# Hybrid S5/NATTEN/PEER layer: a third pair of split weight buffers, and the chunk states laid out chunk by chunk

## The chip, the cores and the metric

The kernel runs on one core of one Trainium2 chip. The metric is the device time of one execution in microseconds, taken as the median of several executions; a profile is one further execution, recorded by the hardware profiler. Engines are named as in the profile: PE (TensorE, matmul; PEld its weight loads), DVE (VectorE), ACT (ScalarE), POOL (GpSimd), SP (SyncE, which issues DMAs). `mm`, `mc`, `kk`, `yy` and `tp` are PSUM banks.

## What is computed

One layer on 512 latent tokens of width 1024, with 256 context tokens, in float32: a modulated RMSNorm; one wide projection `w_in` into u (512), k, v, q (512 each) and two gates (1024 each); a bidirectional S5 state space mixer on u beside a neighbourhood attention on q, k, v; a gated merge; then a PEER layer that gathers experts from tables.

```python
hx = modulate(x, p['norm1_g'], shift1, scale1)
hc = modulate(ctx, p['norm1_g'], mod_c[0], mod_c[1])
px = hx @ p['w_in']
u_x, k_x, v_x, q_x, ga_x, gb_x = jnp.split(px, [COL_K, COL_V, COL_Q, COL_GA, COL_GB], axis=-1)
pc = hc @ p['w_in'][:, :(IN_COLS if with_ctx_out else CTX_COLS)]
y_ssm_x, y_ssm_c = s5_mixer(u_x, u_c, p, with_ctx_out)
branch_a = (s5_glu(y_ssm_x, p) @ p['w_branch_a']).astype(x.dtype)
branch_b = na_mixer(q_x, k_x, v_x, kc, vc, p['na_rpb']) @ p['w_branch_b']
merged = jax.nn.sigmoid(ga_x) * branch_a + jax.nn.sigmoid(gb_x) * branch_b
x = x + gate1 * (merged @ p['w_out'])
x = x + gate2 * peer_ffn(modulate(x, p['norm2_g'], shift2, scale2), ...)
return rms_norm(x, final_g)
```

The S5 mixer is a linear recurrence of 32 groups with 64 complex states each, forward and backward, context tokens first. The kernel cuts the 768 tokens into 96 chunks of 8 (32 of context, 64 latent), makes each chunk's end state, and carries the states from chunk to chunk.

## The kernel before

**Matmuls in split precision.** Every weight tile (128 columns, up to 8 blocks of 128x128) is loaded into `wraw`, copied by ACT into `whi` (rounded to fp32r, L174) and the rest taken by DVE into `wlo` = `wraw` - `whi` (L175). A product is then three matmuls: `whi` with the high part of the input, `whi` with its low part, `wlo` with the high part (L445 to L447; 128x512 for the latent tokens into `mm`, 128x256 for the context into `mc`). `wseq` lists all tiles in the order of use: 16 of `win` (u 0 to 3, k 4 to 7, v 8 to 11, q 12 to 15), then those of the merge in the order of the string MERGE, then the later ones. `w_next` gives out the next tile and, through `w_ahead`, starts the loads two tiles ahead and the split one tile ahead. There are three `wraw` and two each of `whi` and `wlo` (`wbufs`).

**Stages.** (1) u: projections 0 to 3, `u_out` writes them to DRAM in chunk order, `x_load` reads them back as X. (2) Block E, `e_part`: 16 sets of four matmuls from X and the matrices FT, each copied out of PSUM by three ACT copies into E (L552 to L554; forward states in partitions 0 to 63, backward ones in reversed order in 64 to 127). (3) Block K, `k_prep` and `g_outer`: outer products on DVE (`Gc`, L330 to L335), matmuls `kk`, `yy` (L518, L521), ACT copies into `ks` (L524), and six stores each from `ks` to Kd in DRAM on SP's queue (L528 to L530). (4) The sweep, `carry`: 12 calls of four DVE instructions (L612 to L615) that carry the states in E over distances of 1, 2, 4, 8, 16 chunks; beside it PE runs the k, v and q projections, whose results ACT copies into kTC (L563 to L572), `vb`, V (L640) and q (L654). (5) S: four ACT copies of the latent chunks of E (L643, L644). (6) Attention and `y_part`, which uses S. (7) The merge: gates, branches, GLU, beside 32 products `jk` for the second modulation (`mod2`, L816, each with a transfer `wm2`, two buffers; the first modulation's rest on `wm`). (8) PEER.

**Layout of E.** It is [128, 2, 32, 97]: real and imaginary part, group, then chunk, chunk innermost. A carry of distance d = 1, 2, 4 ... reads and writes every 2nd, 4th, 8th ... chunk. The multiplier `lam` is broadcast over the chunks.

**What sets the order.** The whole program is put in order by a scheduler that simulates a timeline (`schedule_with_timeline_sim`); SP's order is written by hand. Each engine runs its own queue in that order. Pools are stacks from the two sides of SBUF: a pool that is opened takes the place of those closed before it, and its first use waits for theirs. `gst2` (with `Gc`, `ks`) is closed at the end of block K; `scp` (with `lam`, `ta`, `tb_`) is opened then.

Of the kernel before, what the change touches and what calls it, by code (L numbers as in the profile page):

```python
# [23 lines left out]
KD = 8  # L24
# [4 lines left out]
G = 32  # L29
# [57 lines left out]
def tile_hybrid(ctx, tc, A, out, dbg=None):  # L87
# [66 lines left out]
    wseq += [("wq", i, KD) for i in range(2 * NH)]  # L154
    wseq += [("puT", j, KD) for j in range(UA, 128)]
    mark = [None]
    wraw, wsp = {}, {}
    wext = {}
    wcnt = {}

    def wtile(kind, dt):
        n, x = wbufs[kind]
        c = wcnt[kind] = wcnt.get(kind, -1) + 1
        if wext and c % (n + x) >= n:
            return wext[0].tile([128, KD, 128], dt, tag=kind, name=kind, bufs=x)
        return wst.tile([128, KD, 128], dt, tag=kind, name=kind, bufs=n)
# [3 lines left out]

    def w_split(raw, kn, eng):
        hi = wtile("whi", F32R)
        lo = wtile("wlo", F32R)
        act.copy(hi[:, :kn], raw[:, :kn])  # L174
        i = eng.tensor_sub(lo[:, :kn], raw[:, :kn], hi[:, :kn].bitcast(F32))  # L175
        if eng is gp:
            mark[0] = i.ins
        return hi, lo

    def w_ahead(load_to, split_to, eng):  # L180
        while wpos[0] < min(load_to, len(wseq)):
            i = wpos[0]
            src, m, kn = wseq[i]
            w = wtile("wraw", F32)
            sy.dma_start(w[:, :kn].rearrange("p k c -> p (k c)"), A[src][m])
            wraw[i] = w
            wpos[0] += 1
        while wpos[1] < min(split_to, len(wseq)):
            i = wpos[1]
            wsp[i] = w_split(wraw.pop(i), wseq[i][2], eng)  # L190
            wpos[1] += 1

    def w_next(want, eng=gp):
# [292 lines left out]
    ecm, ep = open_pool(name="ep", bufs=1, side="right")  # L486
    E = ep.tile([128, 2, G, NCK + 1], F32, name="E")
    dve.memset(E[:, :, :, 0:1], 0.0)

# [54 lines left out]
    def e_part(m):  # L544
        for r in range(2):
            for q in (0, 4):
                g0 = 8 * m + q
                p = bank()
                for i in range(4):
                    pe.matmul(p[:, i * NCK:(i + 1) * NCK], FT[m][:, q + i, r], X[:, g0 + i], start=True, stop=True)  # L550
                pv = p[:, :4 * NCK].rearrange("p (g c) -> p g c", c=NCK)
                act.copy(E[0:64, r, g0:g0 + 4, 1:], pv[0:64])  # L552
                act.copy(E[64:128, r, g0:g0 + 4, 1:1 + CC], pv[64:128, :, CC - 1::-1])
                act.copy(E[64:128, r, g0:g0 + 4, 1 + CC:], pv[64:128, :, NCK - 1:CC - 1:-1])  # L554

# [45 lines left out]
    def carry(l, first, step, n):  # L601

        ta = scp.tile([128, 2, G, 31], F32, name="ta", tag="ta", bufs=1)[:, :, :, 0:n]
        tb_ = scp.tile([128, 2, G, 31], F32, name="tb_", tag="tb_", bufs=1)[:, :, :, 0:n]
        d = 1 << l
        to = E[:, :, :, first:first + (n - 1) * step + 1:step]
        fr = E[:, :, :, first - d:first - d + (n - 1) * step + 1:step]

        def bc(j):
            return lam[l][:, j].rearrange("p r (g o) -> p r g o", o=1).to_broadcast([128, 2, G, n])  # L610

        dve.tensor_tensor(ta, fr, bc(0), op=ALU.mult)  # L612
# [791 lines left out]
```

## Time and profile before

| | |
|---|---|
| median of 3 runs | 1843.59 us (1843.41 to 1844.24) |
| profiled execution, its own time | 1847.01 us |
| its span | 1845.2 us |
| mean granted PE clock of it | 0.968 |
| PE busy | 1724.4 us (93%) |
| DVE busy | 1468.6 us (80%) |
| ACT busy | 782.4 us (42%) |
| POOL busy | 372.9 us (20%) |

The span is the profiled execution from first to last instruction; its own time has the launch around it. A busy PE is one that has a matmul under way; the granted clock says at which part of full speed (2.4 GHz is 1.00, 1.2 GHz 0.50). In the page's list of what ended last PE holds 64% of the span, DVE 18%, DMA 9%. On times of the first stages: blocks E and K lie at about 88 to 133 us, the sweep with the k, v and q projections at 133 to 222, attention to about 311, the merge to about 432.

### The profile page before, as it was taken

What the parts mean: (1) busy time and instruction counts of PE and PEld (TensorE: products, weight loads), DVE (VectorE), ACT (ScalarE), POOL (GpSimd) and SP (SyncE); (2) the same over time, 40 slices, a digit from 0 to 9 for tenths busy, and PEclk for the clock granted to TensorE, in tenths of its full rate; (3) what the DMA queues carried; (4) which work ended last, traced back from release to release, by engine and by line L of the source; (5) the groups of instructions that cost most, each with busy time, mean ns of one, the idle gap of its engine ahead of it and who ended that gap; (6) DMA issues with size and microseconds to landing.
All of it is one profiled execution on the core that took longest, in us unless ns stands there. A gap on an engine that the chain in (4) does not pass through costs nothing.

```text
span 1845.2 us, 27478 instructions
## 1 busy us (share of the span) xinstructions
PE 1724.4 (93%) x9941; PEld 1507.5 (82%) x9941; DVE 1468.6 (80%) x3041; ACT 782.4 (42%) x1220; POOL 372.9 (20%) x304
## 2 busy tenths in 40 slices
PE   5999899899999899995589999999999999999997
PEld 2878677777799799994579899999999999988885
DVE  8889765875689998999888788888878788794455
ACT  6452555432464346665423333333333333333333
POOL 0001000000000000000332344544445444440012
PEclk9999999999999999995699999999999999999998
DMA  8341362885634336765799799999999999994332
GB/s 332 95 134 59 97 170 49 282 285 164 210 130 149 115 121 187 209 196 166 228 392 348 266 344 354 323 340 342 331 337 350 341 328 344 327 337 138 127 114 80
DMA packets 186328, 426.16 MB, mean 231 GB/s; under 512 B 25552, under 2 KB 91216, under 8 KB 186192
## 3 DMA queue, kind: packets, MB, share of 16 engines
q1 hardware_dynamic: 84816, 231.44, 37.1%
q0 software_dynamic: 36864, 134.23, 20.2%
q10 hardware_dynamic: 64512, 58.73, 10.2%
q8 instruction: 78, 1.28, 0.3%
q14 instruction: 58, 0.48, 0.1%
HBM read 388.72 MB, written 35.62 MB: 230 GB/s over the span
## 4 chain that ended last, share of the span: by engine, by line
PE 64%; DVE 18%; DMA 9%; issue 5%; POOL 2%; ACT 2%; SPq 0%; ACTq 0%; DVEq 0%; POOLq 0%
PE acc L1276 8%; PE acc L1275 8%; PE acc L1277 8%; PE kk L447 4%; PE yy L445 4%; PE yy L447 4%; PE yy L446 4%; PE kk L446 4%; PE kk L445 4%; DVE wlo L175 3%; DMA wm<-in_wmodT_dram 3%; PE mm L445 2%; PE mm L447 2%; DMA gu<-in_pu_dram,idx 2%; PE mm L446 2%
## 5 line engine op out<-in xcount | busy, mean ns | idle before, releaser
L174 ACT CAST whi<-wraw 128x1024 fp32r<-128x1024 f32 (+1 forms) x212 | 213.8, 1009 | 222.6 <-PE mm L446 100.4
L1158 POOL DMA_INDIRECT gu<-in_pu_dram,idx x128 | 168.9, 1319 | 598.0 <-PE mm L1142 385.3
L175 DVE TENSOR_TENSOR wlo<-wraw,whi 128x1024 fp32r<-128x1024 f32 (+1 forms) x212 | 247.6, 1169 | 36.1 <-ACT whi L174 35.5
L1158 POOL DMA_INDIRECT gu<-in_pv_dram,idx x128 | 176.8, 1382 | 192.1 <-DVE gacc L1176 165.8
L1176 DVE SCALAR_TENSOR_TENSOR gacc<-gu,av,gacc 128x1024 f32<-128x1024 f32 x127 | 162.7, 1281 | 28.1 <-DMA gu<-in_pv_dram,idx 27.7
L1257 DVE TENSOR_TENSOR wlo<-wraw,whi 128x1024 fp32r<-128x1024 f32 x128 | 157.6, 1232 | 33.5 <-ACT whi L1256 33.0
L1165 DVE SCALAR_TENSOR_TENSOR gj<-gu,hrow 128x1024 bf16<-128x1024 f32 x128 | 156.2, 1220 | 33.9 <-DMA gu<-in_pu_dram,idx 33.8
L447 PE MATMUL kk<-hth,wlo 128*128 128x384 f32 x512 | 174.2, 340 | 3.4 <-DVE wlo L175 3.4
L445 PE MATMUL kk<-hth,whi 128*128 128x384 f32 x512 | 173.4, 339 | 2.4 <-ACT ring L956 2.4
L445 PE MATMUL yy<-hth,whi 128*128 128x384 f32 x512 | 173.0, 338 | 1.5 <-ACT whi L174 1.3
L446 PE MATMUL kk<-htl,whi 128*128 128x384 f32 x512 | 173.1, 338 | 0.0
L447 PE MATMUL yy<-hth,wlo 128*128 128x384 f32 x512 | 173.0, 338 | 0.0
L446 PE MATMUL yy<-htl,whi 128*128 128x384 f32 x512 | 172.4, 337 | 0.0
L1256 ACT CAST whi<-wraw 128x1024 fp32r<-128x1024 f32 x128 | 133.7, 1046 | 59.5 <-PE kk L446 26.7
L1144 ACT ACTIVATE gs<-mm 128x512 f32<-128x512 f32 x96 | 94.1, 1090 | 56.1 <-PE mm L1142 53.1
L447 PE MATMUL mm<-hxh,wlo 128*128 128x512 f32 x256 | 103.3, 404 | 11.4 <-DVE wlo L175 11.4
L445 PE MATMUL mm<-hxh,whi 128*128 128x512 f32 x256 | 101.6, 402 | 5.6 <-ACT whi L174 3.0
L446 PE MATMUL mm<-hxl,whi 128*128 128x512 f32 x256 | 102.5, 400 | 0.0
L447 PEld LDWEIGHTS kk<-hth,wlo 128*128 128x128 f32 x512 | 96.9, 189 | 5.4 <-DVE wlo L175 4.4
L445 PEld LDWEIGHTS kk<-hth,whi 128*128 128x128 f32 x512 | 97.0, 189 | 4.5 <-ACT ring L956 2.7
L445 PEld LDWEIGHTS yy<-hth,whi 128*128 128x128 f32 x512 | 96.4, 188 | 4.6 <-ACT whi L174 1.7
L446 PEld LDWEIGHTS kk<-htl,whi 128*128 128x128 f32 x512 | 97.0, 190 | 1.7
(1912 smaller groups left out, 4258.4 us busy)
## 6 DMA issues: line engine op xcount, KB each, us to landing
wraw<-in_puT_dram SPq DMA_DIRECT2D x128, 512.0 KB
wraw<-in_pv_dram SPq DMA_DIRECT2D x128, 512.0 KB
Gt_d<-gs ACTq DMA_DIRECT2D x24, 1024.0 KB
gch<-Gt_d ACTq DMA_DIRECT2D x32, 768.0 KB
wraw<-in_win_dram SPq DMA_DIRECT2D x32, 512.0 KB
wm<-in_wmodT_dram SPq DMA_DIRECT2D x32, 512.0 KB
wraw<-in_wq_dram SPq DMA_DIRECT2D x32, 512.0 KB
wm<-in_wm_dram SPq DMA_DIRECT2D x16, 512.0 KB
```

The source lines that it names most:

```text
L174: act.copy(hi[:, :kn], raw[:, :kn])
L175: i = eng.tensor_sub(lo[:, :kn], raw[:, :kn], hi[:, :kn].bitcast(F32))
L445: pe.matmul(o, hi[:, k], xh, start=(k == 0), stop=False)
L446: pe.matmul(o, hi[:, k], xl, start=False, stop=False)
L447: pe.matmul(o, lo[:, k], xh, start=False, stop=(k == kn - 1))
L1158: gp.indirect_dma_start(out=u, out_offset=None, in_=A[tab], in_offset=bass.IndirectOffsetOnAxis(ap=ix[:, s:s + 1], axis=0))
L1165: dve.scalar_tensor_tensor(jk, u, 1.0, hrow, op0=ALU.mult, op1=ALU.mult, accum_out=av[:, s:s + 1])
L1176: dve.scalar_tensor_tensor(gacc, u, av[:, s:s + 1], gacc, op0=ALU.mult, op1=ALU.add)
L1257: dve.tensor_sub(lo, w, hi.bitcast(F32))
L1275: pe.matmul(acc[t][half], wh_[:, ts], hi[:, cs], start=(j == 0), stop=False)
L1276: pe.matmul(acc[t][half], wh_[:, ts], lo[:, cs], start=False, stop=False)
L1277: return pe.matmul(acc[t][half], wl_[:, ts], hi[:, cs], start=False, stop=(j == 127))
```

## The change

1. E becomes [128, 97, 2, 32]: chunk first, and a chunk's 64 values (2 parts of 32 groups) side by side. `carry`'s `ta`, `tb_` and the broadcast of `lam` follow. A view Ev = E with the chunk innermost again is what `e_part`'s copies write and the copies to S read.
2. A pool "wx" (8 KB per partition: one `whi`, one `wlo`) is opened on the right side once block K's pools are closed and holds every third split of `win` from tile 5 on; it is closed after the q projections. It is opened again ahead of the merge for the merge's tiles and closed before PEER's pools. While it is open, `w_next` starts loads three and splits two tiles ahead. The raw buffers stay three.
3. `ry` and `rz` of x1_norm get one buffer instead of two.

```diff
+    def wtile(kind, dt, early=False):
         n, x = wbufs[kind]
+        if early and wxp is not None:
+            wcnt[kind] = c = wcnt.get(kind, -1) + 1
+            p = wxp if c % (n + 1) == n else wst
+            return p.tile([128, KD, 128], dt, tag=kind, name=kind, bufs=1 if p is wxp else n)
...
-            wsp[i] = w_split(wraw.pop(i), wseq[i][2], eng)
+            wsp[i] = w_split(wraw.pop(i), wseq[i][2], eng, i < nwx)
...
-        w_ahead(i + 3, i + 2, eng)
+        x = wxp is not None and i + 2 < nwx
+        w_ahead(i + 3 + x, i + 2 + x, eng)
...
-    E = ep.tile([128, 2, G, NCK + 1], F32, name="E")
-    dve.memset(E[:, :, :, 0:1], 0.0)
+    E = ep.tile([128, NCK + 1, 2, G], F32, name="E")
+    Ev = E.rearrange("p c r g -> p r g c")
+    dve.memset(E[:, 0], 0.0)
...
-                act.copy(E[0:64, r, g0:g0 + 4, 1:], pv[0:64])
-                act.copy(E[64:128, r, g0:g0 + 4, 1:1 + CC], pv[64:128, :, CC - 1::-1])
-                act.copy(E[64:128, r, g0:g0 + 4, 1 + CC:], pv[64:128, :, NCK - 1:CC - 1:-1])
+                act.copy(Ev[0:64, r, g0:g0 + 4, 1:], pv[0:64])
+                act.copy(Ev[64:128, r, g0:g0 + 4, 1:1 + CC], pv[64:128, :, CC - 1::-1])
+                act.copy(Ev[64:128, r, g0:g0 + 4, 1 + CC:], pv[64:128, :, NCK - 1:CC - 1:-1])
...
+    wxcm, wxp = open_pool(name="wx", bufs=1, side="right")
+    nwx = 16
     sccm, scp = open_pool(name="scp", bufs=1, side="right")
...
-        ta = scp.tile([128, 2, G, 31], F32, name="ta", tag="ta", bufs=1)[:, :, :, 0:n]
-        tb_ = scp.tile([128, 2, G, 31], F32, name="tb_", tag="tb_", bufs=1)[:, :, :, 0:n]
+        ta = scp.tile([128, 31, 2, G], F32, name="ta", tag="ta", bufs=1)[:, 0:n]
+        tb_ = scp.tile([128, 31, 2, G], F32, name="tb_", tag="tb_", bufs=1)[:, 0:n]
...
-            return lam[l][:, j].rearrange("p r (g o) -> p r g o", o=1).to_broadcast([128, 2, G, n])
+            return lam[l][:, j:j + 1].to_broadcast([128, n, 2, G])
...
-        act.copy(S[0:64, r], E[0:64, r, :, CC:CC + CL])
-        act.copy(S[64:128, r], E[64:128, r, :, CC + CL - 1:CC - 1:-1])
+        act.copy(S[0:64, r], Ev[0:64, r, :, CC:CC + CL])
+        act.copy(S[64:128, r], Ev[64:128, r, :, CC + CL - 1:CC - 1:-1])
...
-    close_pool(sccm, ecm)
+    close_pool(sccm, wxcm, ecm)
+    wxp = None
...
     close_pool(ycm, xscm)
+    wxcm, wxp = open_pool(name="wx", bufs=1, side="right")
+    nwx = [w[0] for w in wseq].index("wq")
...
-        ss, y, z = (x1p.tile([128, 1], F32, tag=n, name=n, bufs=2) for n in ("ss", "ry", "rz"))
+        ss, y, z = (x1p.tile([128, 1], F32, tag=n, name=n, bufs=1 + (n == "ss")) for n in ("ss", "ry", "rz"))
...
     close_pool(wocm, m2cm, mgcm)
+    close_pool(wxcm)
```

The lines after the change are numbered some 6 to 14 higher: L174 and L175 become L180 and L181, L445 to L447 become L452 to L454, L518, L521 and L524 become L526, L529 and L532, L552 to L554 become L560 to L562, L563 to L565 become L571 to L573, L612 to L615 become L622 to L625, L640 becomes L650, L643 and L644 become L653 and L654, L654 becomes L664. Three places show how the scheduler's order moves.

PE at the end of block K, before: between the last `kk` and `yy` matmuls stand projection matmuls of a 2nd and 3rd tile, and after them only a tile's context part (`mc`) is left.

```order
L447 MATMUL mm<-hxh_91,wlo 128x512
L518 MATMUL kk<-Gc,Bp 32x128 x2
L445 MATMUL mm<-hxh_92,whi 128x512
...
L445 MATMUL mm<-hxh_97,whi 128x512
L446 MATMUL mm<-hxl_105,whi 128x512
L447 MATMUL mm<-hxh_97,wlo 128x512
L518 MATMUL kk<-Gc,Bp 32x128 x6
L521 MATMUL kk<-crt,Bb 32x16 x8
L518 MATMUL yy<-Gc,Bp 32x128 x8
L521 MATMUL yy<-crt,Bb 32x16 x8
L445 MATMUL mc<-hc_106,whi 128x256
```

PE at the same place, after:

```order
L454 MATMUL mm<-hxh_97,wlo 128x512
L526 MATMUL kk<-Gc,Bp 32x128 x6
L529 MATMUL kk<-crt,Bb 32x16 x8
L526 MATMUL yy<-Gc,Bp 32x128 x8
L529 MATMUL yy<-crt,Bb 32x16 x8
L526 MATMUL kk<-Gc,Bp 32x128 x8
L529 MATMUL kk<-crt,Bb 32x16 x8
L526 MATMUL yy<-Gc,Bp 32x128 x8
L529 MATMUL yy<-crt,Bb 32x16 x8
L452 MATMUL mm<-hxh_90,whi 128x512
L453 MATMUL mm<-hxl_98,whi 128x512
L452 MATMUL mc<-hc_106,whi 128x256
```

The last four k_prep calls' matmuls now follow each other with no projection matmul between them; the 48 that stood there before come behind the end of the block (72 projection matmuls stand in block K before, 24 after).

ACT at the start of the sweep, before (numbers name single buffers; kTC0 to kTC3 are the four k tiles, `whi_1838` the split of tile 6):

```order
L563 COPY kTC0_1766<-mm_1716 128x8x8
L564 COPY kTC0_1766<-mm_1716 128x8x8
L565 COPY kTC0_1766<-mm_1716 128x8x3x16
L572 COPY kTC0_1766<-mc_1741 128x256
L563 COPY kTC1_1829<-mm_1779 128x8x8
...
L565 COPY kTC2_1892<-mm_1842 128x8x3x16
L174 CAST whi_1838<-wraw_1773 128x1024
```

ACT at the same place, after (`whi_1717` is the split of tile 5, the first in the pool "wx"):

```order
L571 COPY kTC0_1775<-mm_1725 128x8x8
L572 COPY kTC0_1775<-mm_1725 128x8x8
L573 COPY kTC0_1775<-mm_1725 128x8x3x16
L580 COPY kTC0_1775<-mc_1750 128x256
L180 CAST whi_1717<-wraw_1054 128x1024
L571 COPY kTC1_1838<-mm_1788 128x8x8
L572 COPY kTC1_1838<-mm_1788 128x8x8
```

The copies of kTC1 and kTC2, which stood ahead of a split, stand behind this split now. Its place in SBUF is within that of the two `ks` buffers of the closed pool; before, `ta` and `tb_` of the sweep had it.

ACT at the end of the q projections, before (`vb_2242` is the v tile 11, `whi_2338` the last q tile's split):

```order
L174 CAST whi_2303<-wraw_2266 128x1024
L640 COPY V1_1963<-tp_2255 128x3x128
L654 ACTIVATE q0_2264<-mm_2272 64x8x4x16 x2
L174 CAST whi_2338<-wraw_2301 128x1024
L654 ACTIVATE q0_2264<-mm_2307 64x8x4x16 x2
L643 COPY S_737<-E_741 64x2048
L644 COPY S_737<-E_741 64x2048
L643 COPY S_737<-E_741 64x2048
```

ACT at the same place, after (`vb_2177` is tile 10, `vb_2251` tile 11; `whi_2197` the split of tile 13):

```order
L180 CAST whi_2197<-wraw_2121 128x1024
L653 COPY S_737<-E_741 64x2048
L645 COPY vb_2177<-mc_2152 128x256
L654 COPY S_737<-E_741 64x2048
L653 COPY S_737<-E_741 64x2048
L654 COPY S_737<-E_741 64x2048
L650 COPY V0_1971<-tp_2184 128x4x128
L180 CAST whi_2312<-wraw_2275 128x1024
L664 ACTIVATE q0_2273<-mm_2281 64x8x4x16 x2
L650 COPY V1_1972<-tp_2190 128x3x128
L571 COPY vb_2251<-mm_2201 128x8x8
```

The four copies of S moved from behind the first two q tiles' copies to ahead of the copies of tiles 10 to 12.

## Rows read from the trace of the kernel before

**Rows 1.** The page's part 1: busy us (share of the span) and instructions of engines.
```profile
PE 1724.4 (93%) x9941; PEld 1507.5 (82%) x9941; DVE 1468.6 (80%) x3041; ACT 782.4 (42%) x1220; POOL 372.9 (20%) x304
```

**Rows 2.** Windows: stretch, us; busy us of PE, PEld, DVE, ACT, POOL; granted clock; DMA share; GB/s.
```profile
88.00:112.00 24.00, 24.00 (x254) 22.18 (x253) 23.14 (x65) 20.18 (x59) 0.00 (x0) 1.00 0.46 128
112.00:133.40 21.40, 21.40 (x247) 15.21 (x245) 18.35 (x53) 5.71 (x19) 0.00 (x0) 1.00 0.55 163
133.40:222.00 88.60, 78.31 (x415) 67.13 (x415) 74.44 (x97) 35.05 (x68) 5.80 (x24) 0.94 0.22 65
...
311.00:432.00 121.00, 111.86 (x491) 89.00 (x490) 92.73 (x148) 48.02 (x73) 0.00 (x0) 0.97 0.80 260
...
354.00:362.00 8.00, 6.34 (x17) 5.04 (x18) 7.04 (x12) 2.48 (x4) 0.00 (x0) 0.57 0.94 304
```

**Rows 3.** Waits of PE, 130 to 222 us: us in total, times, longest us.
```profile
PE mm L447 <- DVE wlo L175: 6.4, 2, 4.3
```

**Rows 4.** Waits of PE, 311 to 432 us.
```profile
PE mm L447 <- DVE wlo L175: 5.9, 4, 3.3
PE mm L445 <- DVE sg L831: 2.6, 1, 2.6
```

**Rows 5.** Timeline of ACT, block E: start us, us, engine, line, operation, out<-in [idle before].
```profile
109.74 0.47 ACT L552 COPY E<-mm 64x384 f32<-64x384 f32 x1
110.22 0.26 ACT L553 COPY E<-mm 64x128 f32<-64x128 f32 x1
110.39 0.37 ACT L554 COPY E<-mm 64x256 f32<-64x256 f32 x1
```

**Rows 6.** Timeline of PE, blocks E and K and the start of the sweep.
```profile
110.47 0.50 PE L445 MATMUL mm<-hxh,whi 128*128 128x512 f32 x1
110.81 0.39 PE L446 MATMUL mm<-hxl,whi 128*128 128x512 f32 x1
...
112.66 0.40 PE L445 MATMUL mm<-hxh,whi 128*128 128x512 f32 x1
...
140.34 0.28 PE L446 MATMUL mc<-hc,whi 128*128 128x256 f32 x1
140.46 0.28 PE L447 MATMUL mc<-hc,wlo 128*128 128x256 f32 x1
```

**Rows 7.** Groups of DVE by form, 130 to 235 us: count | busy us, mean ns.
```profile
L612 DVE TENSOR_TENSOR ta<-E,lam 128x960 f32<-128x960 f32 x2 | 3.8, 1902 | 0.1
...
L612 DVE TENSOR_TENSOR ta<-E,L 128x1024 f32<-128x1024 f32 x1 | 1.2, 1228 | 6.3 <-DMA Kd<-ks 6.3
...
L612 DVE TENSOR_TENSOR ta<-E,lam 128x512 f32<-128x512 f32 x1 | 1.1, 1068 | 0.0
```

**Rows 8.** Groups of ACT by form, 75 to 340 us.
```profile
L643 ACT COPY S<-E 64x2048 f32<-64x2048 f32 x2 | 3.9, 1934 | 2.6 <-DVE E L615 2.6
...
L534 ACT COPY uT<-mm 128x512 f32<-128x512 f32 x2 | 2.2, 1116 | 8.9 <-DMA X<-Ud 7.3 <-PE mm L447 1.6
...
L640 ACT COPY V<-tp 128x512 f32<-128x512 f32 x4 | 2.4, 590 | 0.5 <-PE tp L639 0.5
```

**Rows 9.** Instructions of line 354: duration ns min/median/max, first and last start us.
```profile
L354 ACT COPY PG<-pw x2: 1079/1101/1123, 22.5 to 23.7; 64x512 f32<-64x512 f32 x2
```

**Rows 10.** Timeline of DVE, ACT and SP's queue (SPq): end of block K, start of the sweep.
```profile
113.44 0.43 DVE L331 TENSOR_TENSOR Gc<-PG,crt 128x256 f32<-128x256 f32 x1 [0.18 <-PE kk L518]
...
134.11 1.13 ACT L524 COPY ks<-yy 32x144 f32<-32x144 f32 x4
...
139.49 0.42 SPq L530 DMA_DIRECT2D Kd<-ks  x1
...
141.11 1.23 DVE L613 TENSOR_TENSOR tb__1615<-E,L 128x1024 f32<-128x1024 f32 x1 [1.51 <-DMA Kd<-ks]
```

**Rows 11.** Timeline of DVE in the merge.
```profile
353.68 1.23 DVE L816 SCALAR_TENSOR_TENSOR jk<-wm,cb 128x1024 bf16<-128x1024 f32 x1 [1.91 <-DMA wm<-in_wmodT_dram]
```

**Rows 12.** Instructions with tile ry, 480 to 540 us: duration ns min/median/max.
```profile
L933 ACT ACTIVATE x<-x,ry x4: 1147/1150/1162, 498.1 to 520.7; 128x1024 f32<-128x1024 f32 x4
```

More of the change, by code (lines that the diff above doesn't have):

```diff
@@ L155, in tile_hybrid @@
     wseq += [("puT", j, KD) for j in range(UA, 128)]
+    nwx = 0
     mark = [None]
@@ L159, in tile_hybrid @@
     wcnt = {}
-    def wtile(kind, dt):
+    wxp = None
+    def wtile(kind, dt, early=False):
         n, x = wbufs[kind]
+        if early and wxp is not None:
+            wcnt[kind] = c = wcnt.get(kind, -1) + 1
+            p = wxp if c % (n + 1) == n else wst
+            return p.tile([128, KD, 128], dt, tag=kind, name=kind, bufs=1 if p is wxp else n)
         c = wcnt[kind] = wcnt.get(kind, -1) + 1
@@ L169, in tile_hybrid, with w_split @@
     wpos = [0, 0, 0]
-    def w_split(raw, kn, eng):
-        hi = wtile("whi", F32R)
-        lo = wtile("wlo", F32R)
+    def w_split(raw, kn, eng, early=False):
+        hi = wtile("whi", F32R, early)
+        lo = wtile("wlo", F32R, early)
         act.copy(hi[:, :kn], raw[:, :kn])
@@ L601, in carry @@
     def carry(l, first, step, n):
-        ta = scp.tile([128, 2, G, 31], F32, name="ta", tag="ta", bufs=1)[:, :, :, 0:n]
-        tb_ = scp.tile([128, 2, G, 31], F32, name="tb_", tag="tb_", bufs=1)[:, :, :, 0:n]
+        ta = scp.tile([128, 31, 2, G], F32, name="ta", tag="ta", bufs=1)[:, 0:n]
+        tb_ = scp.tile([128, 31, 2, G], F32, name="tb_", tag="tb_", bufs=1)[:, 0:n]
         d = 1 << l
-        to = E[:, :, :, first:first + (n - 1) * step + 1:step]
-        fr = E[:, :, :, first - d:first - d + (n - 1) * step + 1:step]
+        to = E[:, first:first + (n - 1) * step + 1:step]
+        fr = E[:, first - d:first - d + (n - 1) * step + 1:step]
         def bc(j):
-            return lam[l][:, j].rearrange("p r (g o) -> p r g o", o=1).to_broadcast([128, 2, G, n])
+            return lam[l][:, j:j + 1].to_broadcast([128, n, 2, G])
         dve.tensor_tensor(ta, fr, bc(0), op=ALU.mult)
-        dve.tensor_tensor(tb_, fr[:, ::-1], bc(1), op=ALU.mult)
+        dve.tensor_tensor(tb_, fr[:, :, ::-1], bc(1), op=ALU.mult)
         dve.tensor_tensor(to, to, ta, op=ALU.add)
@@ L654, in tile_hybrid @@
             act.activation(qT[2 * m + e][s].rearrange("p (j r c) -> p r j c", r=8, c=16), av[s], AF.Copy, scale=0.125)
-    close_pool(sccm, ecm)
+    close_pool(sccm, wxcm, ecm)
+    wxp = None
     ycm, yp = open_pool(name="yp", bufs=1, side="right")
```

## The prediction

> **What bounds the kernel now.** I read the page's busy line first [rows 1]: TensorE is busy 93% of the span, so the time moves only where TensorE idles or runs at its lower clock. The table of windows [rows 2] then tells where that is. In 88 to 112 us (blocks E and K: chunk states and convolution kernels are made) and in 112 to 133.4 us (rest of K) TensorE is full at clock 1.00. From 133.4 to 222 us (the sweep over the states on VectorE, beside the rest of the input projection on TensorE) it is busy 78.3 of 88.6 us at 0.94, so 10.3 us are idle and about 0.06 x 88.6 = 5.3 us go to the clock. From 311 to 432 us (merge) it is busy 111.9 of 121 us at 0.97. The waits say for whom: 6.4 us in two waits for `wlo` in the sweep stretch [rows 3]; in the merge 5.9 us in four waits for `wlo` and 2.6 us for `sg` [rows 4]. The clock row 354:362 [rows 2] shows what such a wait leaves behind: granted 0.57 over 8 us, between the levels of 1.2 and 2.4 GHz, about 3.4 us lost. So there is something to gain: in theory 6.4 us and some clock in the sweep, 5.9 us and perhaps as much again in the merge.
>
> Third, I read ScalarE in 88 to 112 us. It is busy 20.2 us [rows 2], and in the E block its copies stand back to back: L552 at 109.74, L553 at 110.22, L554 at 110.39, which ends at 110.76 [rows 5]. TensorE's next projection tile begins at 110.47 [rows 6], once a bank of E is copied out. So ScalarE's copies are what E goes at, with hardly any slack.
>
> **Part 1: E chunk by chunk, on VectorE.** In the sweep the inner elements now lie side by side. The rows give the price of a stride: 1024 elements at step 2 take 1.23 us (1.2 ns each), 512 at step 4 take 1.07 (2.1 ns), 960 take 1.90 (2.0 ns) [rows 7]. I take about 1.1 ns for all afterwards. There are 8 instructions of 960, 8 of 448, 4 of 512 and 8 of 192, and some of 256 and 64: 8 x 0.83 + 8 x 0.54 + 4 x 0.5 + 8 x 0.24 + about 2 = 17 us less on VectorE. All of it lies beside TensorE's projections, so it is worth nothing by itself. What it does is end the sweep early enough for the copies of S (below).
>
> **Part 2: E chunk by chunk, on ScalarE.** The same turn makes ScalarE's 48 copies into E write at a stride of 256 B, and its 4 copies E to S read so. No copy of before does exactly that. Nearest rows: L534, 128x512 from PSUM with a strided write, 1116 ns; L640, the same size side by side, 590 ns [rows 8]; and L354, a strided read of 64x512, 1101 ns [rows 9]. So a stride costs (1116 - 590) / 512 = 1.03 ns per element. The lower bound is nothing at all (if a 256 B stride should be as cheap as a close one); above, I see nothing dearer. I take 1.03, because writes and reads agree in it.
> The Trainium skill ("Advanced Engine Details and Errata", section "SBUF Cachelines") says that SBUF is reached in lines of 16 bytes and that accesses which each touch another line pay a penalty. The steps of 2 and 4 on VectorE bear it out (two hits to a line at 1.2 ns, one at 2.1); it gives no figure, so the sum goes by the rows, and it speaks against this change on ScalarE as much as for it on VectorE.
> - E: one set is 384 + 128 + 256 = 768 elements, 0.79 us more on its 1.02. The fourteen sets that stand ahead of the copy on which the projection's bank waits give 11.1 us, less about 1.1 us that ScalarE idles, less about 1 us that the banks buffer: TensorE's tile begins not at 110.47 but at about 119.6, 9.1 us later, and TensorE has nothing else in its order. The outer products on VectorE at 113.44 wait for TensorE's `kk` [rows 10] and start at about 122, 8.5 us late. They bind, with 18.35 us of VectorE's work in the 21.4 us of that stretch [rows 2]: block K ends at about 142, not 133.4.
> - S: 4 x 2048 elements, 8.4 us on 7.7, 16.1 us together.
>
> **Part 3: the order.** Until now 72 projection matmuls fill TensorE's gaps in block K; in the changed order only 24 do, and 48 (two tiles' worth) stand behind its end. They cost 48 x 0.23 = 11.0 us (eight steps from 110.81 to 112.66 [rows 6]), now after K and not within it. The first of them needs the tile in the third `whi`, and that buffer's place holds the two `ks` buffers of block K. Its split on ScalarE must so wait until every store Kd<-ks has landed. Before, `ta` and `tb_` of the sweep paid that: `tb_` starts at 141.11 after a wait for Kd<-ks; the last `ks` copies start at 134.11 and the last issue on SP's queue is at 139.49 [rows 10]. In the changed order no filler delays TensorE's last `kk` and `yy`, so the last copy ends not at 135.24 but near 133.9, its six issues (0.42 each) at 136.4, landed 1.15 us after (139.49 + 0.42 to 141.06): 137.6. With 8.5 us of shift and 1.04 us of split TensorE restarts at 147.2; were the stores as late as before, at 141.1 + 8.5 + 1.04 = 150.6. I take 148.5. Behind that split on ScalarE stand the kTC copies of the next tiles; they have nothing to copy until TensorE runs.
>
> **Part 4: two tiles ahead.** From the restart TensorE has the stretch's old work, 78.3 us busy less 5.3 us of clock = 73.0, and the 11.0: 84.0 us (in rows: 11 tiles x 24 x 0.23 + 7 x 24 x 0.12, the 0.12 from 140.34 and 140.46 [rows 6], = 80.9, and some transposes and first scores). The waits for `wlo`, 6.4 us, and the clock loss after them go. Against that: about 2 us at the lower clock on the restart, and 1.5 after the stand that follows (the one at 354:362 lost 3.4 [rows 2]).
> And the S copies stand elsewhere: before, behind the copies of q; now right behind the split `whi` of tile 13, ahead of the copies of tile 10's and 11's `vb`, of V and of q. That split waits for the end T of tile 10's context matmuls. From T ScalarE needs 1.05 (split) + 16.1 (S) + 0.4 + 0.6 + 1.05 + 1.2 + 0.5 + 1.0 = 21.9 us until tile 11's `vb` is ready for the transposes that stand next on TensorE; TensorE has 48 x 0.23 + 24 x 0.12 + 0.4 = 14.3 us of work until then. So it stands for about 7 us. T is 148.5 + 7 x 5.5 + 6 x 2.9 + 3 = 207.4; the sweep (from 147, some 51 us with its splits) is over by 198, so S doesn't wait for it.
> End of the stretch: 148.5 + 84.0 + 2 + 7 + 1.5 = 243.0 instead of 222: **+21 us**.
>
> **Part 5: the merge.** Splits two ahead start `wlo` a tile earlier. VectorE there is paced by the products `jk`, 32 of them, each of which waits for its transfer `wm` (1.91 us at 353.68, [rows 11]); `wlo` stands between them in the same queue, so it comes earlier by places in the order, and not by less work. Bounds: nothing, and 5.9 + 2.6 + 3.4 (the clock at 354:362) = 11.9 us. The wait for `sg` isn't a split's, so I take the `wlo` waits alone: **-6 us**.
>
> **Part 6: the rest.** `ry` and `rz` with one buffer let a tile's root wait for the previous tile's scaling, 1.15 us at L933 [rows 12], three times at most 1.2 and beside TensorE's transposes: 0, at most +2. Loads three ahead cost nothing, since the raw buffers remain three. After the merge the order is as before.
>
> Sum: 21 - 6 = +15 on the profiled execution's 1847.0 us: 1862. That execution stands 3.4 us above the median 1843.6, so the median goes to **1858 us** (0.8% slower).
>
> **Rivals.**
> A, faster: ScalarE's strided copies cost no more than before, because a write from 64 partitions is held by PSUM and not by SBUF's stride. For it: no row has exactly this copy. Against: L534 and L354, both at twice the price. It decides from the duration of L560 to L562 (0.47/0.26/0.37 kept). Then E and K end as before, TensorE restarts at 137.6 + 1.0 = 138.6, has 84.0 + 2 to do and hardly a stand at S (8.4 us less there), say 1: it ends at 225.6, +4, less 6 to 12 in the merge: about 1839.
> B, slower still: the sweep keeps its 73 us (138.37 to 211.6), and the S copies at the head of ScalarE's queue wait for it and hold `vb`, V and q behind them. S then starts at about 220.5, not at 208.5, 12 us later: 1871. For it: S waited 2.6 us for E before too. Against: the price of step 2 beside step 4 [rows 7].
> C, no change: it does part of what it says, with half the strided price, or a restart without the wait for `ks` and the merge's whole 12 us: 21 - 8.5 - 12 = about 0, so 1842 to 1850, 1846 taken.
>
> **How the numbers follow.** Forecast 0.62, with its own range 1850 to 1867 (merge 0 to -12, restart +-2, S +-3); A 0.14; B 0.10; C 0.14, two thirds of it within 0.2%. A measurement tells about 0.2%, 3.7 us, from no change (1839.9 to 1847.3). Faster: A's 0.14 and a little of C, 0.15. Same: 0.09. Slower: 0.76. The range 1842 to 1872 leaves out A and a tail above B, 0.2 together.
>
> **What would show it.** L560 at about 0.87 us and S (L653) at about 4.0 us; TensorE idle some 9 us near 112 to 119 and again in K; a restart near 148 on `mm` behind the split from `wraw`; sweep instructions of 960 near 1.1 us; no `wlo` waits between 148 and 200, and a stand of about 7 us before the last two q tiles; the merge 4 to 8 us shorter. I am wrong if L560 stays at 0.47, if TensorE has other work in its order while E is copied, or if the merge gives back more than 12 us.

## The result, and the profile after

The changed kernel took 1870.84 us (median of 4 runs, 1865.6 to 2874.28; before, beside it: 1843.5). The run of 2874 us had a granted clock of 0.556 and is left out of the ratio, which the other three (median 1866.92) make: 1.0139 (95% interval 1.0121 to 1.0157), 1.4% slower, 26 us. The profiled execution took 1866.92 us with a span of 1865.2, 20 us above that of before. A later measurement of the same kernel gave 1.0125 (1.0091 to 1.0159). The prediction said 1858, with 1842 to 1872 as its range: the sign and the places are as forecast, the size was 11 us short by the ratio (which puts the kernel at 1869, above the forecast's own 1850 to 1867), and 5 us by the profiled execution (1862 to 1866.9).

The windows of after, which answer to [rows 2], with the stretches moved to where the stages now lie (columns as there: PE, PEld, DVE, ACT, POOL, clock, DMA share, GB/s):

```profile
88.00:122.00 34.00, 31.41 (x285) 27.38 (x285) 25.17 (x69) 31.14 (x60) 0.00 (x0) 0.90 0.36 110
122.00:142.00 20.00, 11.34 (x190) 7.36 (x180) 16.95 (x48) 6.93 (x24) 0.63 (x8) 0.72 0.46 137
142.00:152.00 10.00, 3.62 (x11) 3.00 (x12) 6.55 (x13) 2.54 (x7) 0.29 (x4) 0.54 0.25 67
152.00:200.00 48.00, 48.00 (x274) 41.92 (x273) 42.72 (x78) 11.16 (x28) 4.22 (x10) 1.00 0.15 49
200.00:250.00 50.00, 44.13 (x241) 35.69 (x241) 16.17 (x18) 33.54 (x40) 0.65 (x5) 0.93 0.38 112
...
340.00:460.00 120.00, 112.35 (x484) 90.40 (x483) 94.41 (x148) 47.27 (x69) 0.00 (x0) 0.97 0.78 261
```

ACT is now busy 31.1 of 34 us around block E, and PE, which was full in blocks E and K, is idle 2.6, then 8.7, then 6.4 us in the first three windows, at a clock that falls to 0.54. Then, from 152 to 200, where before waited for `wlo` [rows 3], it is full at 1.00: that part of the intention works, though by the shorter sweep and not by the third pair, as the experiments show. From 200 to 250 it idles 5.9 us again.

Groups of ACT by form, 75 to 360 us, against [rows 5, 8]:

```profile
L560 ACT COPY E<-mm 64x384 f32<-64x384 f32 x16 | 13.2, 826 | 0.3
L562 ACT COPY E<-mm 64x256 f32<-64x256 f32 x16 | 10.3, 645 | 0.0
L653 ACT COPY S<-E 64x2048 f32<-64x2048 f32 x2 | 7.8, 3902 | 0.0
L654 ACT COPY S<-E 64x2048 f32<-64x2048 f32 x2 | 7.6, 3815 | 0.0
L561 ACT COPY E<-mm 64x128 f32<-64x128 f32 x16 | 6.1, 380 | 0.2
```

The copies into E went from 0.47, 0.26, 0.37 to 0.83, 0.38, 0.65 us, those to S from 1.93 to 3.9.

Timeline of PE, against [rows 6]: the first projection tile after E, two stands in block K, and the restart.

```profile
118.19 0.80 PE L452 MATMUL mm<-hxh,whi 128*128 128x512 f32 x1 [0.15 <-ACT E L562]
...
131.92 0.86 PE L526 MATMUL yy<-Gc,Bp 128*32 128x128 f32 x10 [3.49 <-DVE Gc L339]
...
137.36 0.86 PE L526 MATMUL kk<-Gc,Bp 128*32 128x128 f32 x10 [3.36 <-DVE Gc L339]
...
148.38 0.79 PE L452 MATMUL mm<-hxh,whi 128*128 128x512 f32 x1 [7.09 <-ACT whi L180]
```

Timeline of ACT and of SP's queue ahead of that restart, against [rows 10]: the last `ks` copies, the last store, the split of tile 5.

```profile
141.39 1.13 ACT L532 COPY ks<-yy 32x144 f32<-32x144 f32 x4 [1.55 <-PE yy L529]
...
145.69 0.42 SPq L538 DMA_DIRECT2D Kd<-ks  x1
...
147.28 1.04 ACT L180 CAST whi<-wraw 128x1024 fp32r<-128x1024 f32 x1 [3.76 <-DMA Kd<-ks]
```

What stood under `tb_` before stands under PE now. Waits of PE, 88 to 250 us (us in total, times, longest), and then ACT's timeline where the second of these falls:

```profile
PE mm L452 <- ACT whi L180: 7.1, 1, 7.1
PE tp L649 <- ACT vb L572: 5.3, 1, 5.3
```

```profile
207.05 1.05 ACT L180 CAST whi<-wraw 128x1024 fp32r<-128x1024 f32 x1 [1.66 <-PE mc L453]
208.00 3.91 ACT L653 COPY S<-E 64x2048 f32<-64x2048 f32 x1
...
212.20 3.88 ACT L654 COPY S<-E 64x2048 f32<-64x2048 f32 x1
216.10 3.90 ACT L653 COPY S<-E 64x2048 f32<-64x2048 f32 x1
220.00 3.75 ACT L654 COPY S<-E 64x2048 f32<-64x2048 f32 x1
223.78 0.59 ACT L650 COPY V<-tp 128x512 f32<-128x512 f32 x1
```

For 15.8 us, from 208.0 to 223.8, ACT copies S and lets only one short copy through, and the `vb` copies for which PE's transposes wait are behind.

DVE's part came as meant. Groups of DVE by form, 135 to 215 us, against [rows 7]:

```profile
L622 DVE TENSOR_TENSOR ta<-E,L 128x1984 f32<-128x1984 f32 x2 | 4.5, 2225 | 0.1
...
L622 DVE TENSOR_TENSOR ta<-E,lam 128x960 f32<-128x960 f32 x2 | 2.3, 1156 | 0.0
```

960 elements take 1.16 instead of 1.90 us; 1984, at step 2 before, take what they took. Added over all 64 instructions of the sweep's four lines (`carry` is called 16 times, not 12), 63.4 us became 48.6.

Waits of PE in the merge, 321 to 485 us, against [rows 4]:

```profile
PE mm L452 <- ACT whi L180: 3.6, 1, 3.6
PE mm L454 <- DVE wlo L181: 3.3, 1, 3.3
PE mm L452 <- ACT ah L865: 0.8, 1, 0.8
```

7.7 us of waits where before had 8.9 (the two of [rows 4] and one of 0.4). The waits of DVE's products for their transfers, before and then after, are as long as they were:

```profile
DVE jk L816 <- DMA wm<-in_wmodT_dram: 18.6, 20, 1.9
```

```profile
DVE jk L829 <- DMA wm<-in_wmodT_dram: 18.6, 14, 2.1
```

(The profile leaves buffer numbers out of names, so `wm2` stands there as `wm`.)

### The profile page after: what moved, and what is told of

It reads as the page before. It is cut to its first block, busy times and chain, and to the rows that moved or that the text cites. A ratio compares the mean times of both kernels' runs of the same rounds, so it can differ in the third digit from the quotient of the medians.

```text
span 1865.2 us, 27490 instructions
## 1 busy us (share of the span) xinstructions
PE 1731.1 (93%) x9941; PEld 1513.1 (81%) x9941; DVE 1455.4 (78%) x3041; ACT 800.7 (43%) x1220; POOL 368.3 (20%) x304
## 4 chain that ended last, share of the span: by engine, by line
PE 78%; DVE 12%; DMA 4%; ACT 3%; issue 2%; POOL 0%; SPq 0%; ACTq 0%; DVEq 0%; POOLq 0%
PE acc L1289 9%; PE acc L1290 9%; PE acc L1291 9%; PE kk L454 5%; PE yy L454 5%; PE kk L452 5%; PE kk L453 5%; PE yy L452 5%; PE yy L453 5%; PE mm L452 4%; PE mm L453 4%; PE mm L454 4%; DVE wlo L181 2%; DMA wm<-in_wmodT_dram 2%; PE tp L734 1%
## 5 line engine op out<-in xcount | busy, mean ns | idle before, releaser
L180 ACT CAST whi<-wraw 128x1024 fp32r<-128x1024 f32 (+1 forms) x212 | 213.7, 1009 | 202.9 <-PE mm L453 72.1
L181 DVE TENSOR_TENSOR wlo<-wraw,whi 128x1024 fp32r<-128x1024 f32 (+1 forms) x212 | 247.3, 1168 | 53.9 <-ACT whi L180 50.2
L1172 POOL DMA_INDIRECT gu<-in_pu_dram,idx x128 | 164.6, 1286 | 607.1 <-PE mm L1156 393.1
L1271 DVE TENSOR_TENSOR wlo<-wraw,whi 128x1024 fp32r<-128x1024 f32 x128 | 157.6, 1232 | 31.7 <-ACT whi L1270 31.1
L1190 DVE SCALAR_TENSOR_TENSOR gacc<-gu,av,gacc 128x1024 f32<-128x1024 f32 x127 | 162.7, 1281 | 23.0 <-DMA gu<-in_pv_dram,idx 22.7
L454 PE MATMUL kk<-hth,wlo 128*128 128x384 f32 x512 | 174.9, 342 | 3.8 <-DVE wlo L181 3.8
L452 PE MATMUL kk<-hth,whi 128*128 128x384 f32 x512 | 173.8, 339 | 2.4 <-ACT ring L969 2.4
L452 PE MATMUL yy<-hth,whi 128*128 128x384 f32 x512 | 172.8, 338 | 1.5 <-ACT whi L180 1.3
L454 PE MATMUL yy<-hth,wlo 128*128 128x384 f32 x512 | 173.0, 338 | 0.1
L452 PE MATMUL mm<-hxh,whi 128*128 128x512 f32 x256 | 104.1, 412 | 12.8 <-ACT whi L180 12.6
L454 PE MATMUL mm<-hxh,wlo 128*128 128x512 f32 x256 | 102.9, 403 | 3.3 <-DVE wlo L181 3.3
L454 PEld LDWEIGHTS kk<-hth,wlo 128*128 128x128 f32 x512 | 97.3, 190 | 5.8 <-DVE wlo L181 4.8
L452 PEld LDWEIGHTS kk<-hth,whi 128*128 128x128 f32 x512 | 97.5, 190 | 4.6 <-ACT ring L969 2.7
L452 PEld LDWEIGHTS yy<-hth,whi 128*128 128x128 f32 x512 | 96.2, 188 | 4.4 <-ACT whi L180 1.7
```

Of the source, the lines that this page charges most:

```text
L452: pe.matmul(o, hi[:, k], xh, start=(k == 0), stop=False)
L454: pe.matmul(o, lo[:, k], xh, start=False, stop=(k == kn - 1))
L1172: gp.indirect_dma_start(out=u, out_offset=None, in_=A[tab], in_offset=bass.IndirectOffsetOnAxis(ap=ix[:, s:s + 1], axis=0))
L1190: dve.scalar_tensor_tensor(gacc, u, av[:, s:s + 1], gacc, op0=ALU.mult, op1=ALU.add)
L1271: dve.tensor_sub(lo, w, hi.bitcast(F32))
```

## The experiments

The theory was that three things cost: the stride of ACT's copies into E; the third pair's place, which keeps tile 5 out of block K and ties it to the stores from `ks`; and the copies of S, by their stride and their place in ACT's queue. The rivals were that one of the first two is the whole loss. Since the times of one kernel scatter by several us, the stages are compared in this table, read from each kernel's instruction lists (start of the first matmul of E, of the last score matmul, of the last gate's activation; us from the span's start). The last column is what is left to the span's end. Each ratio is to runs of before taken beside that kernel (medians 1841.97 to 1846.33), so ratios are compared and not times of different rows.

| kernel | time, ratio (95%) | first E | last score | E to score | last gate | score to gate | rest |
|---|---|---|---|---|---|---|---|
| before | 1843.59 | 88.3 | 298.6 | 210.3 | 463.6 | 165.0 | 1381.6 |
| after | 1.0139 (1.0121 to 1.0157) | 89.8 | 321.5 | 231.7 | 483.4 | 161.9 | 1381.8 |
| after_again | 1.0125 (1.0091 to 1.0159) | 88.5 | 320.8 | 232.3 | 485.0 | 164.2 | 1382.2 |
| layout_only | 1.0038 (1.0022 to 1.0053) | 90.4 | 309.3 | 218.9 | 473.0 | 163.7 | 1380.4 |
| pair_only | 1.0099 (1.0073 to 1.0125) | 88.5 | 311.8 | 223.3 | 475.3 | 163.5 | 1379.1 |
| after_from7 | 1.0069 (1.0045 to 1.0092) | 89.8 | 309.5 | 219.7 | 476.7 | 167.2 | 1377.7 |
| pair_from7 | 1.0041 (1.0028 to 1.0055) | 90.6 | 305.0 | 214.4 | 470.0 | 165.0 | 1379.0 |
| after_Edense | 1.0118 (1.01 to 1.0136) | 89.7 | 314.1 | 224.4 | 479.1 | 165.0 | 1385.7 |
| after_Sdense | 1.0099 (1.0076 to 1.0121) | 89.3 | 311.8 | 222.5 | 475.8 | 164.0 | 1380.9 |
| layout_Eg | 0.9991 (0.9975 to 1.0008) | 89.8 | 299.9 | 210.1 | 464.3 | 164.4 | 1381.1 |
| layout_Eg_Sg | 0.9953 (0.9938 to 0.9967) | 89.7 | 291.7 | 202.0 | 454.4 | 162.7 | 1380.3 |
| after_from7_Eg_Sg | 0.9997 (0.9984 to 1.001) | 89.6 | 295.0 | 205.4 | 455.9 | 160.9 | 1378.4 |
| pair_merge_only | 1.0007 (0.9987 to 1.0026) | 89.8 | 302.0 | 212.2 | 465.2 | 163.2 | 1379.4 |
| layout_Eg_Sg_wm3 | 0.992 (0.989 to 0.9951) | 88.4 | 291.4 | 203.0 | 446.1 | 154.7 | 1384.2 |

The scatter can be read in it: pair_merge_only has the code of before up to the last score and is 1.9 us longer there; the rest, in which hardly anything differs, goes from 1377.7 to 1385.7.

**The layout alone.** The pool "wx" is never opened, and `ry` and `rz` have two buffers again; all else as changed.

```diff
-    wxcm, wxp = open_pool(name="wx", bufs=1, side="right")
-    nwx = 16
...
-    close_pool(sccm, wxcm, ecm)
-    wxp = None
+    close_pool(sccm, ecm)
```

> Only the new layout of E; two pairs of split buffers, and the order of before. My theory (the loss has two parts of like size: the strided copies on ScalarE, and the third pair that holds tile 5 back until block K's stores have landed): projection after E begins 8 to 9 us late (near 119), block K ends near 142 and has its 72 filler matmuls, the sweep is 17 us shorter so that the waits for wlo (6.4 us) go, S takes 4.0 us a copy: 1847 to 1854 us. Rival 1 (the stride is the whole loss): 1862 to 1867. Rival 2 (the third pair is the whole loss, the slower copies are hidden): 1836 to 1844.

1852.74 us, within my theory's range; E to score is 8.6 us longer than before. The waits for `wlo` are gone from PE's waits, 88 to 345 us. In their place stands one that I had not priced, behind S, in spite of the old order (waits of PE of this kernel, as above):

```profile
PE mm L718 <- ACT q L662: 7.8, 1, 7.8
```

The first score waits for the copies of the later q tiles, which stand behind the four copies of S, as they did before; but these take 3.9 us each now.

**The pair alone.** E in the old layout; third pair as changed.

> Only the third pair, in both stages; E in the old layout. My theory: E and block K end as in the kernel before (133), but 48 matmuls stand behind K's end and TensorE restarts only near 139 to 140, and the copies of S, ahead of v's and q's, wait for the sweep of old length (end near 211), so TensorE stands some 10 us before the last q tiles: 1853 to 1860 us. Rival 1 (the stride is the whole loss): 1836 to 1842. Rival 2 (the third pair is the whole loss): 1862 to 1868.

1860.75 us, just above my theory's range: 13.0 us more than before in E to score. With blocks E and K at their old speed the late restart is there, and a second stand ahead of the last q tiles. Timeline of PE, then its waits (88 to 345 us), then the timeline of ACT of this kernel:

```profile
139.86 0.79 PE L452 MATMUL mm<-hxh,whi 128*128 128x512 f32 x1 [7.31 <-ACT whi L180]
```

```profile
PE mm L454 <- DVE wlo L181: 5.2, 1, 5.2
```

```profile
207.18 1.94 ACT L653 COPY S<-E 64x2048 f32<-64x2048 f32 x1 [7.28 <-DVE E L625]
```

So the wait of 7 us at the restart is the pair's and not the layout's. The dense S copies, being early in the queue, do wait for the long sweep, but PE's second stand isn't theirs as my theory had it: PE waits 5.2 us for a `wlo`, which stands behind the same sweep in DVE's queue. Neither rival holds: each half costs alone. In E to score 8.6 + 13.0 = 21.6 us, and both together 21.4. That is no breakdown, though: the waits differ (for `q` behind S with the layout alone, for `wlo` with the pair alone, for `vb` behind S with both).

**The third pair from tile 7 on.** The changed kernel with one index moved.

```diff
+    wxm = [1]
...
-            p = wxp if c % (n + 1) == n else wst
+            p = wxp if c % (n + 1) == wxm[0] else wst
```

> The changed kernel with one thing else: the first split that goes into the third pair is tile 7's and not tile 5's (then 10, 13), so that tiles 5 and 6 have buffers free of block K's. My theory: the 48 filler matmuls are back within block K, the restart near 145 has no 7 us wait for Kd<-ks, S stands behind q again; the 9 us at E remain: 1846 to 1854 us, at least 12 less than the changed kernel. Rival 1 (the stride is the whole loss): 1862 to 1868, as the changed kernel. Rival 2 (the third pair costs by its existence, by DMA or by places in the queues, not by which tile is first in it): also 1862 to 1868.

1856.92 us, 12 us less in E to score than the changed kernel (219.7 against 231.7), which is nearly all that the pair had cost there. Of the restart's wait 1.9 us are left. The time is 3 us above my range: I had priced no wait behind S, and there is one of 7.0, now for `q` (waits of PE, 88 to 345 us):

```profile
PE mm L722 <- ACT q L665: 7.0, 1, 7.0
...
PE mm L453 <- ACT whi L181: 1.9, 1, 1.9
```

**The pair from tile 7 on, in the old layout.**

> The third pair from tile 7 on, E in the old layout: the change without the two parts that I hold to be the loss. My theory: E and block K as before, filler within K, splits of the sweep stretch earlier: the 6.4 us of waits for wlo and some clock go, and about 2 us in the merge: 1833 to 1841 us, faster than both. Rival: VectorE's old sweep stands ahead of the wlo splits in its queue whatever the buffers, so the waits stay: 1842 to 1846 us.

1851.33 us, with E to score 4.1 us longer: a miss, slower than before by more than its interval and slower than the rival's range. The pair doesn't remove the waits (waits of PE, 88 to 345 us):

```profile
PE mm L455 <- DVE wlo L182: 5.5, 2, 3.4
```

Before has 7.8 us of waits for `wlo` there, and 5.2 in pair_merge_only, which has the same code up to the last score. With the other four of that stretch they make 12.9 us, where before has 11.7: `wlo` waits in DVE's queue for the sweep, not for a buffer. Where the rest of the 4.1 us comes from isn't shown; 2 of them are within the scatter.

**E side by side in the changed kernel.** ACT writes the same number of elements to E's bytes taken as [part, group, chunk]; the sweep then reads values of other chunks.

```diff
+    Ef = E.rearrange("p c r g -> p (c r g)").rearrange("p (r g c) -> p r g c", r=2, g=G)
...
-                act.copy(Ev[0:64, r, g0:g0 + 4, 1:], pv[0:64])
+                act.copy(Ef[0:64, r, g0:g0 + 4, 1:], pv[0:64])
```

> The changed kernel, except that ScalarE writes E side by side (into the same bytes taken as part, group, chunk), so the sweep reads values from the wrong chunks; number, size and order of the instructions are as in the changed kernel, with one small memset more. My theory (the stride of the 48 writes is what E costs): the three copies fall from 0.83, 0.38 and 0.65 us to 0.47, 0.26 and 0.37, projection after E begins near 110, block K ends near 133, TensorE restarts near 140: 8 to 9 us less than the changed kernel, 1856 to 1860 us. Rival (the copies are bound by the read from PSUM, or something else fills E): under 3 us less, 1864 to 1867.

The copies are back at their old durations (groups of ACT by form):

```profile
L562 ACT COPY E<-mm 64x384 f32<-64x384 f32 x16 | 7.6, 472 | 1.2 <-PE mm L560 0.9
```

and E to score is 7.3 us shorter, as my theory had it. The time isn't: 1865.09 us, in the rival's range. The merge and the rest of this execution are 3.1 and 3.9 us longer than in the changed kernel's, nearly all that the copies gave. Whether that is scatter alone isn't settled (1385.7 is the highest of the table's last column, 165.0 lies in the upper half of the other); the stage is.

**S side by side in the changed kernel.** The same with the four reads of S, which then gets values of other chunks.

```diff
-        act.copy(S[0:64, r], Ev[0:64, r, :, CC:CC + CL])
+        act.copy(S[0:64, r], Ef[0:64, r, :, CC:CC + CL])
```

> The changed kernel, except that the four copies to S read E side by side (so S gets values of the wrong chunks); all else as there. My theory: a copy takes 1.93 us instead of 3.9, TensorE's wait of 5.3 us behind them goes and with it a microsecond of clock: 5 to 7 us less than the changed kernel, 1859 to 1863 us. Rival (their place in the queue is the cost, not their length): 0 to 2 us less, 1864 to 1867.

1860.32 us and 9.2 us less in E to score. The copies take 1.93 us, and the wait of 5.3 us is gone from PE's list. So S cost by its length, at that place.

**The copies turned.** Two pairs of buffers, as with the layout alone. If a stride costs where it is written, the copies can put the four groups of a set side by side, with the chunk outside, and S can follow E's layout.

```diff
-                act.copy(Ev[0:64, r, g0:g0 + 4, 1:], pv[0:64])
+                act.copy(E[0:64, 1:, r, g0:g0 + 4], pc[0:64])
...
-    S = xs_.tile([128, 2, G, CL], F32, name="S")
+    S = xs_.tile([128, 2, CL, G], F32, name="S")
...
-        act.copy(S[0:64, r], Ev[0:64, r, :, CC:CC + CL])
+        act.copy(S[0:64, r], E[0:64, CC:CC + CL, r])
```

Here pc is the bank as [partition, chunk, group]; the copies of the backward half go alike, and `y_part` takes S[:, r, :, g].

> Only the new layout (two pairs of buffers), with the copies turned: into E with the chunk outside and the set's four groups inside (16 bytes side by side, read from PSUM at a step of 96), and S laid out chunk by chunk too, so that its copies read and write 32 groups side by side and TensorE reads S at a step of 32. My theory: both sides count by how many neighbours are touched in a row; E's copies come back to 0.5 to 0.6 us for 384 elements, S to 2.0, the wlo waits stay away: 1833 to 1840 us, faster than before. Rival: a stride costs on the reading side in PSUM as much as on the writing side, so E's copies stay at 0.8: 1843 to 1848.

1834.83 us, ratio 0.9953 (0.9938 to 0.9967): faster than both kernels, within my range. Groups of ACT by form, and of PE's weight loads, 200 to 300 us:

```profile
L560 ACT COPY E<-mm 64x384 f32<-64x384 f32 x16 | 7.6, 472 | 1.3 <-PE mm L558 0.9
...
L651 ACT COPY S<-E 64x2048 f32<-64x2048 f32 x2 | 3.8, 1906 | 0.0
```

```profile
L690 PEld LDWEIGHTS yy<-gt,S 128*64 128x64 f32 x128 | 10.9, 194 | 0.8 <-issue 0.8
```

Every copy is as fast as in the kernel before, the sweep is short, PE's waits for `wlo` (88 to 345 us) are down from 7.8 to 1.9 us, and E to score is 8.3 us shorter than before. The loads of S as weights, at a step of 32, went from 137 to 194 ns, but PE loads weights beside its matmuls: the mean of these went only from 276 to 284 ns, 0.5 us over all 128.

> The layout alone with the turned copies into E, S as in the changed kernel (copies of 3.9 us that read at a stride). My theory: E is as fast as before, the wlo waits are gone, and the S copies, which stand behind two q copies and ahead of the others, let TensorE stand 5 to 8 us before the scores: 1838 to 1844 us, 4 to 8 more than with S laid out chunk by chunk too (1834.8). Rival (S is hidden): 1833 to 1836.

This kernel, with the turned copies into E alone, took 1844.84 us, 0.9991 (0.9975 to 1.0008), just above my range: E to score 210.1, 8.1 more than with S. PE waits 7.8 us for `q` again. So S isn't hidden, and what the short sweep gives is lost to S unless S is turned too.

> The same copies turned, with the third pair from tile 7 on and in the merge. My theory: once the sweep is short, the third pair has no wait left to remove in the sweep stretch, and in the merge the pace is that of the transfers wm: within 3 us of the kernel with the layout alone, 1833 to 1842. Rival (the pair is worth its waits in the merge): 5 us or more faster than that kernel.

With the third pair beside the turned copies: 1840.53 us, 0.9997 (0.9984 to 1.001), within the range that I gave, but 6 us more than without it, which neither side had. In the profiled execution, the fastest of ten (1836.02), E to score is 3.4 us longer and the merge 1.8 shorter; where the longer times of the others come from isn't shown. The pair is in no case a gain.

**The merge.** The third pair there alone, before's code otherwise, and then the turned kernel with one more buffer for the transfers of the second modulation:

```diff
-        w = m2p.tile([128, D], F32, tag="wm2", name="wm2", bufs=2)
+        w = m2p.tile([128, D], F32, tag="wm2", name="wm2", bufs=3)
```

> The kernel before with the third pair in the merge alone (old layout, two pairs up to there). The prediction gave this -6 us (waits for wlo gone): 1836 to 1839. My theory now: VectorE's products jk go at the pace of the transfers wm and the splits stand between them, so the pair moves waits from one instruction to another; from the last score to the last gate (165.0 us before) it takes 162 to 167: 1841 to 1846 us.

> The layout with turned copies, and three buffers instead of two for the transfers wm2 of the merge (tag wm2; 4 KB per partition more). If the waits of jk for wm (18 us in the merge) are what paces VectorE there and are due to a load that starts too late: jk's waits fall by half or more, the merge (last score to last gate, 162.7 us) is 4 to 10 us shorter, 1824 to 1832 us. If the transfers go at the rate that the DMA queues give: under 2 us, 1832 to 1837.

pair_merge_only: 1846.51 us beside 1846.33 for before, 1.0007 (0.9987 to 1.0026): nothing. From score to gate it takes 163.2 us, the eight other executions with a pair in the merge 160.9 to 167.2, the four with two pairs and two `wm2` buffers 162.7 to 165.0. Waits of DVE from score to gate, first of pair_merge_only, then of the turned kernel with two and with three `wm2`:

```profile
DVE jk L826 <- DMA wm<-in_wmodT_dram: 19.3, 15, 2.6
```

```profile
DVE jk L824 <- DMA wm<-in_wmodT_dram: 18.0, 17, 2.2
```

```profile
DVE jk L824 <- DMA wm<-in_wmodT_dram: 2.9, 3, 1.1
```

The products' waits are as long with the pair as without it, and a third buffer for `wm` takes most of them away. PE's own waits there fall from 9.2 to 3.2 us, and score to gate from 162.7 to 154.7 us, shorter than in any other kernel of the table. The time is 1832.03 us, 0.992 (0.989 to 0.9951): faster than before, and the lowest of all kernels here, though the interval overlaps that of two `wm2` (0.9938 to 0.9967). In its profiled execution the rest was 3.9 us longer, so half of the stage's gain didn't reach the end of that execution.

> The changed kernel once more, beside the others. If its second profile shows the same delays as its first (projection after E at 118, restart at 148, wait of 5.3 us behind S, last score at 321), the scatter of its times lies after the merge: 1862 to 1872 us.

1870.51 us. The second profile of the changed kernel has the same delays (restart's wait 7.0, wait behind S 5.3, last score at 320.8); its merge is 2.3 us longer than in the first. E starts 1.3 us earlier in it, and so do the first projection (116.77) and the restart (146.91), which stand as far behind E's start as in the first profile.

## Why the prediction held, and where it did not

- ACT's stride (part 2). 1.03 ns per element was taken; the 48 copies grew from 17.7 to 29.6 us, 11.9 for 12.6 predicted, and those to S from 7.7 to 15.4, for 16.1. Projection began at 118.19 (119.6), the last `ks` copies ended at 142.5 (142.4). What this delays was put too high: counted from E's first matmul, projection came 6.2 us later than before (28.4 for 22.2 us), and the isolated price of the stride in E is 7.3 us (after_Edense), for 9.1. Why less isn't shown. TensorE didn't stand 9 us there either, only 2.6 us from 88 to 122, at a clock of 0.90.
- The order and the restart (part 3). 148.38 for 148.5, by the mechanism named: the split of tile 5 waits for the last Kd<-ks. That it is right to 0.1 us is luck: E began 1.5 us later than before (89.8 for 88.3), which the change doesn't explain, since E's start goes from 88.3 to 90.6 over the table; counted from there the restart came at 58.6 us, 1.6 earlier than forecast. after_from7 shows that its cost, with the filler, is 12 us.
- The S copies (part 4). 3.90 and 3.82 us (4.0), a wait of 5.3 us (7). The q copies ended at 243.8 + 0.6 (stretch's end 243.0).
- The sweep (part 1). 14.8 us less for 17. Part 1 gave it no worth by itself and part 4 gave the end of the `wlo` waits to the third pair; the runs show it the other way round. With the pair and the old sweep PE still waits 5.2 and 5.5 us for `wlo` (pair_only, pair_from7), with the short sweep and no pair 0, 2.5 and 1.9 (layout_only, layout_Eg, layout_Eg_Sg), and layout_Eg_Sg, which keeps the short sweep and none of the costs, is 8.3 us shorter in E to score.
- The stretch as a whole. E to score grew by 21.4 us, the prediction's +21, so the sum is right though terms were off by 1 to 3 us either way. Undone one at a time, the pair's place, S's stride and E's stride give back 12.0, 9.2 and 7.3 us, 28.5 together. That this is some 7 us more than 21.4 fits what the short sweep is worth (8.3), but no run shows that they add in this way. The last score is 22.9 us later, as E began 1.5 us later too.
- **The step that failed is part 5, the merge: -6 us.** The argument beside it was right (jk paces DVE by `wm`, `wlo` stands between), but the value was taken from PE's waits for `wlo`, the follower, and not from DVE's, the leader: those for `wm` are 18.6 us before and after. PE's waits changed places, 7.7 us for 8.9. Score to gate is 3.1 us shorter in this execution and 0.8 in after_again; pair_merge_only, 1.8 us shorter in the stage and nothing in time, shows no gain clear of the scatter. The lower bound, nothing, was the better value.
- The rest (part 6) is 1381.8 us for 1381.6: nothing, as said. On the profiled execution the 5 us that the sum was short are thus 3 of the merge, 1.5 of E's later start and 0.6 of the other two.
- The remaining 6 us between the profiled execution and the ratio are taken for scatter: the three runs behind it were 1865.6, 1866.9 and 1874.8, and the profiled one was of the lower two. What sets it isn't known. The prediction subtracted 3.4 us because the profiled execution of before stood above its median; for the changed kernel that went the other way.
- Rival A fell with the copies' durations, B with the sweep's end (S started at 208.0 without waiting for DVE), C with all its parts: the full price of the stride, the restart's wait, and the merge.

## What to carry to other kernels

When a layout is turned for one engine, price every other engine's accesses to the same tile, above all those in a stage without slack; then look for a loop order of the copies that keeps a few neighbours together on the side that is written. A further buffer helps only what waits for a buffer: ask what the waiting instruction stands behind in its queue, and what memory the new buffer takes over, since its first user inherits the last user's stores. Look for the gain of a paced stage in the pace-maker's wait and not in those of who follows it, and take it as a bound from above: a third buffer for `wm` took away 15.1 us of `jk`'s waits, and the stage got 8.0 us shorter.

## What was not expected of the hardware

- A copy that reads PSUM at a step of 96 elements and writes four neighbours at a time is as fast as one with both sides dense: 472 ns for 64x384 in both, against 826 with single elements at 256 B in SBUF. The price was on SBUF's side, and four values of 4 bytes side by side pay none of it.
- Weight loads of 64 columns at a step of 32 elements took 194 ns instead of 137; nearly hidden here, since the matmuls beside them took 284 instead of 276 ns.
- What lies behind the merge took 1377.7 to 1385.7 us (last column of the table) though the kernels hardly differ there, a scatter as large as some effects in question; so the stages had to be compared by the traces.
